# The expert numbers of a PEER selection: from 128 one-column lookups to step comparisons on 64 columns

## The chip, the cores and the metric

The kernel runs on one core of a Trainium2 chip. The metric is the device time of one execution in microseconds (us); smaller is better. The kernel before was run three times for it: 3990.93 us is the median, 3989.17 the lowest and 3995.62 the highest.

## The reference, cut to what matters

The model is a decoder of two layers for 512 tokens of width 1024. Each layer has a mixer (HGRN2 and S5 branches) and then a PEER part: eight heads per token choose 16 of 16384 experts each, an expert is one row of a table U and one of a table V. The choice is what the change touches:

```
s = einsum('thpd,hpnd->thpn', q, keys32)              # 128 scores for each of two key halves
s1_v, s1_i = top_k(s[:, :, 0, :], 16)
s2_v, s2_i = top_k(s[:, :, 1, :], 16)
cand_v = s1_v[..., :, None] + s2_v[..., None, :]      # 256 candidates per head
cand_i = s1_i[..., :, None] * 128 + s2_i[..., None, :]
top_v, top_j = top_k(cand_v, 16)
idx = take_along_axis(cand_i, top_j)                  # the expert numbers
gate = softmax(top_v)
act = gelu(einsum('thkd,td->thk', u_tab[idx], hb))
out = einsum('thkd->td', gate * act, v_tab[idx])
```

## The kernel before, in words

The 512 tokens are handled in four blocks of 128, tokens on partitions. For the first 384 tokens the kernel does not gather expert rows: it multiplies the tokens by the whole table U and by the whole table V, as dense matmuls, and weighs the products between them with a matrix of 128 by 128 gates per token, which is nearly all zero. For the last 128 tokens it gathers the chosen rows by indirect DMA, issued on POOL (`gather`, L957), 128 times from U and 128 times from V, through three buffers.

A layer's PEER part (`peer`, L819) has these steps in the order of the program:

- Scores (`scores`, L833): for 16 key halves a matmul, then `top16` on VectorE for each block of tokens, which leaves the 16 best values in `sv` and their numbers in `sx`.
- Selection (`select(tb)`, L847): of the 256 pairs per head only 50 can be among the best 16; `CAND` lists how many second-half partners each of the 16 first-half ranks has (16, 8, 5, 4, 3, 2, 2, 2 and eight times 1), `COFF` where each group begins. `cv` holds the 50 sums of scores, `ci` the 50 sums of codes (first number times 128 plus second number). `top16` finds the 16 best of `cv` per head and their positions `tj`. Then, for each of 8 heads and 16 choices, one instruction (L876) compares the numbers 0 to 49 with the position, multiplies by the 50 codes and accumulates: the result is the chosen code. Shift and mask part it into the two numbers, which go to `fx` with the gates. The block of the gathered tokens is selected first, then the other three in turn.
- Builds (`build`, L907): for four tokens at a time, VectorE makes one-hot matrices P and Q in fp16 (L921, L923, L927), eight matmuls multiply them (L933, L934), and ACT copies the 4 gate matrices to `stg`; each 48 tokens are stored to DRAM (`sW`, L939). There are 32 builds per block, 96 in all.
- U (`dense_U`, L795): 128 times a 512 KB piece of table U is loaded, split on ACT and VectorE into two parts (`whi` L114, `wlo` L116), and multiplied in 24 matmuls (L132 to L134) with the tokens; the result goes to DRAM (`sA`). In the program, one U follows every second build, and the rest of U comes after the builds. Behind each U stands one step of the gathers: a gather, then a product with the token's row on VectorE (L967), later the sum over V rows (`gacc`, L978).
- V (L1041 to L1043): 128 pieces of table V are loaded and split in the same way; `sA` and `sW` are read back, multiplied on VectorE (L1028), and fed to 24 matmuls each, which accumulate in all eight PSUM banks. In the first layer the tables of the next layer's mixer are prepared beside this (`next_layer`).

The order on each engine isn't the order of the program. The kernel is scheduled by a planner that simulates the engines with its own costs and takes, on each engine, what is ready and comes first in the program; U's and V's loads and splits are moved ahead by a fixed priority. Every engine then works through its own list in that order, and waits where an input isn't there.

Of the kernel before, what the change touches and what calls it, by code (L numbers as in the profile page):

```python
# [4 lines left out]
F32 = mybir.dt.float32  # L5
F32R = mybir.dt.float32r
F16 = mybir.dt.float16
I32 = mybir.dt.int32
U32 = mybir.dt.uint32
U8 = mybir.dt.uint8  # L10
AF = mybir.ActivationFunctionType
OP = mybir.AluOpType
# [4 lines left out]
T = 512  # L17
# [19 lines left out]
CAND = [16, 8, 5, 4, 3, 2, 2, 2] + [1] * 8  # L37
NCAND = sum(CAND)
COFF = [sum(CAND[:i]) for i in range(16)]


def trunk(tc, a, dbg=None, layers=L, n_i2=128):
    nc = tc.nc
    V, S, G, TE = nc.vector, nc.scalar, nc.gpsimd, nc.tensor
    uid = [0]

    def nm(s):
        uid[0] += 1
        return f"{s}{uid[0]}"
# [3 lines left out]
    cst = ctx.enter_context(tc.tile_pool(name="cst", bufs=1))  # L53
# [6 lines left out]
    def ptile(shape, tag):  # L60
        return psp.tile(shape, F32, tag=tag, name=nm(tag), bufs=PB[tag])
# [16 lines left out]
    iof = cst.tile([128, 128], F32, name="iof")  # L78
# [16 lines left out]
    V.tensor_tensor(eye4, ident[:, 0:32], ident[:, 32:64], op=OP.add)  # L95
    V.tensor_tensor(eye4, eye4, ident[:, 64:96], op=OP.add)
    V.tensor_tensor(eye4, eye4, ident[:, 96:128], op=OP.add)


    def load_raw(src, eng=None):  # L100
# [299 lines left out]
    def s5_maps(l, sm, keep, pool, tags):  # L400
        E = V
        br, bi, tmp = (pool.tile([128, 32, 16], F32, tag=t, name=nm(t), bufs=1) for t in tags)
        nc.sync.dma_start(br, a["bre"][l])
        nc.sync.dma_start(bi, a["bim"][l])
        bb = [keep.tile([128, 32, 16], F32, name=nm("bb")) for _ in range(2)]
        zrb, zib = (z[:, :, None].to_broadcast([128, 32, 16]) for z in sm["z"])
        E.tensor_tensor(bb[0], zrb, br, op=OP.mult)
        E.tensor_tensor(tmp, zib, bi, op=OP.mult)
        E.tensor_tensor(bb[0], bb[0], tmp, op=OP.subtract)
        E.tensor_tensor(bb[1], zrb, bi, op=OP.mult)  # L410
        E.tensor_tensor(tmp, zib, br, op=OP.mult)
        E.tensor_tensor(bb[1], bb[1], tmp, op=OP.add)
        cc_ = [keep.tile([128, 32, 16], F32, name=nm("cc")) for _ in range(2)]
        nc.sync.dma_start(cc_[0], a["cre"][l])
        nc.sync.dma_start(cc_[1], a["cim"][l])
        S.activation(cc_[1], cc_[1], AF.Copy, scale=-1.0)
        sm.update(bb=bb, cc=cc_)
# [7 lines left out]
    def pack_tile(pool):  # L425
        t = pool.tile([128, PK], F32, name=nm("pk"))
        G.memset(t, 0.0)
        return t
# [55 lines left out]
    def mixer(l, h):  # L484
# [4 lines left out]
        fx = hctx.enter_context(tc.tile_pool(name=f"fx{l}", bufs=1))  # L489
# [9 lines left out]
        if l == 0:  # L499
            s5_maps(l, sm, fx, hp, ("w1", "w2", "w3"))  # L500
            pk0 = pack_tile(fx)
        dcol = fx.tile([128, 32], F32, name=nm("dcol"))
        for j in range(4):
            nc.sync.dma_start(dcol[32 * j:32 * j + 32, :], a["dsk"][l])
# [235 lines left out]
        fx = mctx.enter_context(tc.tile_pool(name=f"gx{l}", bufs=1))  # L740
# [78 lines left out]
    def peer(l, h, rows, gp):  # L819
        pctx = ExitStack()  # L820
        rp = pctx.enter_context(tc.tile_pool(name=f"rp{l}", bufs=2))
# [4 lines left out]
        def top16(val, idx, src, work):  # L826
            V.max(val[:, 0:8], src)
            V.max_index(idx[:, 0:8], val[:, 0:8], src)
            V.match_replace(work, val[:, 0:8], src, NEG)
            V.max(val[:, 8:16], work)  # L830
            V.max_index(idx[:, 8:16], val[:, 8:16], work)

        def scores(p, ps):  # L833
# [9 lines left out]
            for tb in range(NB):  # L843
                wk = rp.tile([128, 128], F32, tag="wk", name=nm("wk"))
                top16(sv[:, tb, p], sx[:, tb, p], s[:, tb], wk)

        def select(tb):  # L847
            val = sv[:, tb].rearrange("p (h s) k -> p h s k", s=2)
            idf = rp.tile([128, 16, 16], F32, tag="idf", name=nm("idf"), bufs=1)
            V.tensor_copy(idf, sx[:, tb])  # L850
            idv = idf[:].rearrange("p (h s) k -> p h s k", s=2)
            V.tensor_scalar(idv[:, :, 0, :], idv[:, :, 0, :], 128.0, None, op0=OP.mult)
            cv = rp.tile([128, 8, NCAND], F32, tag="cv", name=nm("cv"), bufs=1)
            ci = rp.tile([128, 8, NCAND], F32, tag="ci", name=nm("ci"), bufs=1)
            for src, dst in ((val, cv), (idv, ci)):
                for r in range(5):
                    n = CAND[r]
                    V.tensor_tensor(dst[:, :, COFF[r]:COFF[r] + n], src[:, :, 0, r:r + 1].to_broadcast([128, 8, n]),
                                    src[:, :, 1, 0:n], op=OP.add)
                V.tensor_tensor(dst[:, :, COFF[5]:COFF[8]].rearrange("p h (r b) -> p h r b", b=2),  # L860
                                src[:, :, 0, 5:8, None].to_broadcast([128, 8, 3, 2]),
                                src[:, :, 1, None, 0:2].to_broadcast([128, 8, 3, 2]), op=OP.add)
                V.tensor_tensor(dst[:, :, COFF[8]:], src[:, :, 0, 8:16],
                                src[:, :, 1, 0:1].to_broadcast([128, 8, 8]), op=OP.add)
            tv = rp.tile([128, 8, 16], F32, tag="tv", name=nm("tv"), bufs=1)
            tj = rp.tile([128, 8, 16], U32, tag="tj", name=nm("tj"), bufs=1)
            for hh in range(8):
                wk = rp.tile([128, NCAND], F32, tag="wk2", name=nm("wk2"))
                top16(tv[:, hh], tj[:, hh], cv[:, hh], wk)
            tf = rp.tile([128, 8, 16], F32, tag="tf", name=nm("tf"), bufs=1)  # L870
            V.tensor_copy(tf, tj)
            code = rp.tile([128, 8, 16], F32, tag="code", name=nm("code"), bufs=1)
            for hh in range(8):
                for k in range(16):
                    jk = rp.tile([128, NCAND], F32, tag="jk", name=nm("jk"))
                    V.scalar_tensor_tensor(jk, iof[:, 0:NCAND], tf[:, hh, k:k + 1], ci[:, hh], op0=OP.is_equal,  # L876
                                           op1=OP.mult, accum_out=code[:, hh, k:k + 1])
            cint = rp.tile([128, 128], I32, tag="cint", name=nm("cint"), bufs=1)
            V.tensor_copy(cint, code[:].rearrange("p h k -> p (h k)"))
            ii = rp.tile([128, 2, 128], I32, tag="ii", name=nm("ii"), bufs=1)  # L880
            V.tensor_scalar(ii[:, 0], cint, 7, None, op0=OP.logical_shift_right)
            V.tensor_scalar(ii[:, 1], cint, 127, None, op0=OP.bitwise_and)
            fx = rp.tile([128, 3, 128], F32, tag="fx", name=nm("fx"), bufs=1)
            V.tensor_copy(fx[:, 0:2], ii)

            gv = fx[:, 2].rearrange("p (h k) -> p h k", h=8)
            V.tensor_tensor(gv, tv, tv[:, :, 0:1].to_broadcast([128, 8, 16]), op=OP.subtract)
            S.activation(fx[:, 2], fx[:, 2], AF.Exp)
            zs = rp.tile([128, 8], F32, tag="zs", name=nm("zs"), bufs=1)
            V.tensor_reduce(zs, gv, axis=mybir.AxisListType.X, op=OP.add)  # L890
            V.reciprocal(zs, zs)
            V.scalar_tensor_tensor(gv, gv, GATE, zs[:, :, None].to_broadcast([128, 8, 16]), op0=OP.mult, op1=OP.mult)
            if tb == NB - 1:
                return fx
            pt = ptile([128, 3, 128], "pc")
            for i in range(3):
                TE.transpose(pt[:, i], fx[:, i], ident)
            st = rp.tile([128, 2, 128], F16, tag="slot", name=nm("slot"))
            S.activation(st, pt[:, 0:2], AF.Copy)
            gh = rp.tile([128, 2, 128], F16, tag="gh", name=nm("gh"))  # L900
            V.tensor_copy(gh[:, 0], pt[:, 2])
            V.tensor_tensor(gh[:, 1], pt[:, 2], gh[:, 0], op=OP.subtract)
            return st, gh
# [96 lines left out]
        for p in range(16):  # L1000
            scores(p, first[3 + p] if p < 3 else dense(a["wq"][l, p], h))
        steps[0] = gather_steps(select(NB - 1))
        for tb in range(NB - 1):
            sel = select(tb)
# [48 lines left out]
        def spilled(i):  # L1053
            w = wv(i)
            A = vp.tile([128, TD], F32, tag="A", name=nm("A"), bufs=3)
            nc.sync.dma_start(A, sA[l][i])
            return w, gated(i, A)

        n_end = max(n1 - VB, 0)
        for i in range(n_end):  # L1060
            w, g = spilled(i)
# [31 lines left out]
    for k in ("adab", "n1g", "n2g", "glub"):  # L1093
        sh = a[k].shape
# [12 lines left out]
    for j in range(J):  # L1107
        m = cst.tile([128, 2], F32, name=nm("m"))
        for k in range(2):
            t = ad0.tile([128, D], F32, tag="ada", name=nm("ada"))  # L1110
# [35 lines left out]
    for l in range(layers):  # L1146
        h = norm_mod(gain1[l], shift1[l], ssq, G if l == 0 else None)
# [72 lines left out]
```

## Time and profile before

| | |
|---|---|
| median of three runs | 3990.93 us |
| the profiled execution | 3988.25 us, of which 3986.4 us are the span from the first to the last instruction |
| TensorE (PE) busy | 3737.9 us, 94% |
| VectorE (DVE) busy | 3270.8 us, 82% |
| ScalarE (ACT) busy | 1577.6 us, 40% |
| GpSimd (POOL) busy | 883.7 us, 22% |
| mean granted TensorE clock | 0.967 |
| L876 in all | 1024 pairs, 223.9 us for the comparisons and 81.8 for the accumulator reads |

Busy times count an instruction from its start to its end. Instructions of one engine overlap by a little, since one starts while the one before drains, so the sum of two groups can exceed the time in which they ran. Matmul ends are modelled: a TensorE that is busy throughout may still do fewer matmuls per microsecond than in another stretch, so counts (x) are read beside busy times. [...]

### The profile page before, as it was taken

To read this page: it belongs to the slowest core of one execution; us is meant where nothing else is said; L and a number is where in the kernel's file an instruction comes from. 1 tells how busy PE (TensorE), PEld (TensorE's weight loads), DVE (VectorE), ACT (ScalarE), POOL (GpSimd) and SP (SyncE) were. 2 spreads that over 40 slices of the span, in tenths; PEclk is the share of its full clock that TensorE was granted. 3 is DMA by queue.
4 is the path that set the end of the run, shared out by engine and by line. 5 is a ranking of instruction groups with operands and counts; after the bars stand their busy time and mean duration, and the time that the engine had idled before them with its cause. 6 is when DMAs were issued, how large, how long until landed. Compare 5 with 4: busy or idle time off the path is not lost.

```text
span 3986.4 us, 62595 instructions
## 1 busy us (share of the span) xinstructions
PE 3737.9 (94%) x21878; PEld 3500.6 (88%) x21878; DVE 3270.8 (82%) x9052; ACT 1577.6 (40%) x2510; POOL 883.7 (22%) x1139
## 2 busy tenths in 40 slices
PE   6999999999999766889999999999999998699998
PEld 5888878999999766888998888789999997699998
DVE  6998787999898889988757777869998988778874
ACT  3454543334343323334434444533334433233332
POOL 7454100022222433341000000000232223332210
PEclk9999999999999778999999999999999998799999
DMA  5222372488898899998743343723799998999984
GB/s 198 71 65 79 117 230 91 131 296 304 321 320 314 289 327 343 364 345 292 273 146 110 120 141 124 253 87 119 270 316 319 319 321 305 324 345 345 348 296 132
DMA packets 371212, 947.55 MB, mean 238 GB/s; under 512 B 36096, under 2 KB 187712, under 8 KB 368848
## 3 DMA queue, kind: packets, MB, share of 16 engines
q1 hardware_dynamic: 250144, 572.74, 42.5%
q0 software_dynamic: 73952, 268.56, 19.6%
q10 hardware_dynamic: 46800, 102.26, 6.7%
q8 instruction: 172, 2.82, 0.3%
q14 instruction: 144, 1.18, 0.1%
HBM read 814.44 MB, written 128.97 MB: 237 GB/s over the span
## 4 chain that ended last, share of the span: by engine, by line
PE 65%; DVE 16%; DMA 11%; issue 4%; ACT 2%; POOL 2%; ACTq 0%; SPq 0%; DVEq 0%; POOLq 0%
PE mm L133 11%; PE mm L132 11%; PE mm L134 11%; DVE wlo L116 3%; DMA gr<-v,idi 3%; PE mm L1042 2%; PE mm L1043 2%; PE mm L1041 2%; DMA gr<-ur,idi 2%; DVE jk L876 2%; DMA ada<-ada 2%; PE pa L1043 2%; PE pa L1042 2%; PE pb L1042 2%; PE pb L1043 2%
## 5 line engine op out<-in xcount | busy, mean ns | idle before, releaser
L114 ACT ACTIVATE whi<-raw 128x1024 fp32r<-128x1024 f32 x688 | 728.6, 1060 | 1354.1 <-PE mm L133 772.8
L133 PE MATMUL mm<-alo,whi 128*128 128x384 f32 (+1 forms) x3360 | 1213.7, 362 | 13.6 <-DVE alo L123 13.4
L134 PE MATMUL mm<-ahi,wlo 128*128 128x384 f32 (+1 forms) x3360 | 1214.1, 362 | 9.4 <-DVE wlo L116 9.1
L132 PE MATMUL mm<-ahi,whi 128*128 128x384 f32 (+1 forms) x3360 | 1213.0, 363 | 6.4 <-ACT ahi L229 5.6
L116 DVE TENSOR_TENSOR wlo<-raw,whi 128x1024 fp32r<-128x1024 f32 x688 | 840.2, 1222 | 254.5 <-ACT whi L114 239.1
L133 PEld LDWEIGHTS mm<-alo,whi 128*128 128x128 f32 x3360 | 636.0, 189 | 64.2 <-DVE alo L123 14.7
L134 PEld LDWEIGHTS mm<-ahi,wlo 128*128 128x128 f32 x3360 | 636.2, 189 | 61.1 <-DVE wlo L116 12.4
L132 PEld LDWEIGHTS mm<-ahi,whi 128*128 128x128 f32 x3360 | 636.6, 190 | 56.8 <-ACT ahi L229 7.1
L957 POOL DMA_INDIRECT gr<-ur,idi x256 | 278.1, 1086 | 1438.1 <-DVE jk L876 384.0
L957 POOL DMA_INDIRECT gr<-v,idi x256 | 362.2, 1415 | 662.7 <-DVE gacc L978 526.0
L978 DVE SCALAR_TENSOR_TENSOR gacc<-gr,gate,gacc 128x1024 f32<-128x1024 f32 x254 | 324.5, 1278 | 51.1 <-DMA gr<-v,idi 50.3
L1041 PE MATMUL mm<-gh,whi 128*128 128x384 f32 x768 | 227.3, 343 | 112.1 <-ACT whi L114 48.4
L967 DVE SCALAR_TENSOR_TENSOR gr<-gr,rows 128x1024 f32<-128x1024 f32 x256 | 311.0, 1217 | 17.6 <-DMA gr<-ur,idi 17.1
L1042 PE MATMUL mm<-gl,whi 128*128 128x384 f32 x768 | 260.9, 342 | 11.1 <-DVE gl L1032 11.0
L1043 PE MATMUL mm<-gh,wlo 128*128 128x384 f32 x768 | 255.9, 339 | 0.2 <-DVE wlo L116 0.2
L1041 PEld LDWEIGHTS mm<-gh,whi 128*128 128x128 f32 x768 | 142.5, 191 | 116.1 <-ACT gh L1030 66.0
L933 PE MATMUL pa<-Q,P 128*128 128x128 f16 x768 | 197.7, 296 | 43.7 <-DVE Q L927 41.1
L1030 ACT ACTIVATE gh<-A 128x384 fp32r<-128x384 f32 x256 | 132.1, 519 | 268.7 <-DVE A L1028 216.8
L876 DVE SCALAR_TENSOR_TENSOR jk<-iof,tf,ci 128x50 f32<-128x50 f32 x1024 | 223.9, 263 | 0.0
L935 ACT ACTIVATE stg<-pa 128x512 f32<-128x512 f32 x192 | 114.4, 598 | 223.3 <-PE pa L934 191.0
L934 PE MATMUL pa<-Q,P 128*128 128x128 f16 x768 | 187.9, 295 | 1.0
L1028 DVE TENSOR_TENSOR A<-A,W 128x384 f32<-128x384 f32 x256 | 139.2, 552 | 57.1 <-DMA A<-sA 52.0
(410 smaller groups left out, 6573.9 us busy)
## 6 DMA issues: line engine op xcount, KB each, us to landing
raw<-u SPq DMA_DIRECT2D x256, 512.0 KB
raw<-v SPq DMA_DIRECT2D x256, 512.0 KB
raw<-win SPq DMA_DIRECT2D x112, 512.0 KB
ada<-ada SPq DMA_DIRECT2D x96, 512.0 KB
sA<-uo ACTq DMA_DIRECT2D x256, 192.0 KB
sW<-stg ACTq DMA_DIRECT2D x64, 768.0 KB
A<-sA SPq DMA_DIRECT2D x256, 192.0 KB
W<-sW SPq DMA_DIRECT2D x64, 768.0 KB
```

The lines of the kernel that those rows point to most:

```text
L114: S.activation(hi, raw, AF.Copy)
L116: V.tensor_tensor(lo, raw, hi[:].bitcast(F32), op=OP.subtract)
L132: TE.matmul(ps, hi[:, w], ah, start=(j == 0), stop=False)
L133: TE.matmul(ps, hi[:, w], al, start=False, stop=False)
L134: TE.matmul(ps, lo[:, w], ah, start=False, stop=(j == J - 1))
L876: V.scalar_tensor_tensor(jk, iof[:, 0:NCAND], tf[:, hh, k:k + 1], ci[:, hh], op0=OP.is_equal, op1=OP.mult, accum_out=code[:, hh, k:k + 1])
L957: G.indirect_dma_start(out=g[:], out_offset=None, in_=tab, in_offset=bass.IndirectOffsetOnAxis(ap=ids[:, s_:s_ + 1], axis=0))
L967: V.scalar_tensor_tensor(g, g, 1.0, rows, op0=OP.mult, op1=OP.mult, accum_out=dot[:, s_:s_ + 1])
L978: V.scalar_tensor_tensor(acc_, g, gate[:, s_:s_ + 1], acc_, op0=OP.mult, op1=OP.add)
L1041: TE.matmul(ps, w[0][:, c], g[0], start=first, stop=False)
L1042: TE.matmul(ps, w[0][:, c], g[1], start=False, stop=False)
L1043: TE.matmul(ps, w[1][:, c], g[0], start=False, stop=last)
```

## The change

The 128 lookups per block, the codes `ci` and the integer arithmetic behind them go. Instead the two expert numbers are worked out from the position j of a chosen candidate among the 50. For 64 columns at once (four heads of 16 choices; two calls per selection), in fp16:

- the first-half rank is the number of group beginnings (COFF) that j has reached; the first number is the first entry plus the sum, over the 15 steps, of (j >= COFF) times the difference of neighbouring entries;
- the second-half rank is j minus the sum of the sizes (CAND) of the groups passed; the second number is the sum, over 16 ranks, of (rank equal) times the entry.

The sums over 15 or 16 rows are trees of additions that halve the number of rows. Constants are kept as pairs of equal values, so that a repeated operand still has runs of two fp16 values. The working rows are taken from the buffers of tag `s`, which the scores use before. The copy `second` is on ACT, all else on VectorE; the 30 memsets of the constants are on POOL, ahead of the first mixer.

```diff
+    thr = cst.tile([128, 15, 2], F16, name="thr")
+    cnd = cst.tile([128, 15, 2], F16, name="cnd")
+    rnk = cst.tile([128, 16, 2], F16, name="rnk")
+
+    def rank_tables():
+        V.tensor_copy(rnk, iof[:, 0:16, None].to_broadcast([128, 16, 2]))
+        for r in range(1, 16):
+            G.memset(thr[:, r - 1], float(COFF[r]))
+            G.memset(cnd[:, r - 1], float(CAND[r - 1]))
...
+        def ranks(iv, j, o0, o1):
+            j = j.rearrange("p h k -> p (h k)")
+            def work(n):
+                return rp.tile([128, T], F32, tag="s", name=nm("s"))[:].bitcast(F16)[:, 0:64 * n].rearrange(
+                    "p (r x) -> p r x", r=n)
+            def pairs(t, n):
+                return t[:, :, None, :].to_broadcast([128, n, 32, 2])
+            def twos(w):
+                return w.rearrange("p r (a b) -> p r a b", b=2)
+            def total(w, n, o):
+                while n > 2:
+                    m = (n + 1) // 2
+                    V.tensor_tensor(w[:, 0:n - m], w[:, 0:n - m], w[:, m:n], op=OP.add)
+                    n = m
+                V.tensor_tensor(o, w[:, 0], w[:, 1], op=OP.add)
+            def gate_rows(w, t, n):
+                sh = [128, n * 4, 8, 2]
+                v = w.rearrange("p r (h a b) -> p (r h) a b", h=4, b=2)
+                V.tensor_tensor(v, v, t[:].rearrange("p r h b -> p (r h) b")[:, :, None, :].to_broadcast(sh), op=OP.mult)
+            step = rp.tile([128, 15, 4, 2], F16, tag="step", name=nm("step"), bufs=1)
+            two = [128, 4, 15, 2]
+            V.tensor_tensor(step[:].rearrange("p r h b -> p h r b"), iv[:, :, 0, 1:16, None].to_broadcast(two),
+                            iv[:, :, 0, 0:15, None].to_broadcast(two), op=OP.subtract)
+            second = rp.tile([128, 16, 4, 2], F16, tag="second", name=nm("second"), bufs=1)
+            S.activation(second[:].rearrange("p r h b -> p h r b"), iv[:, :, 1, :, None].to_broadcast([128, 4, 16, 2]),
+                         AF.Copy)
+            ge, w = work(15), work(15)
+            V.tensor_tensor(twos(ge), twos(j[:, None].to_broadcast([128, 15, 64])), pairs(thr, 15), op=OP.is_ge)
+            V.tensor_tensor(twos(w), twos(ge), pairs(cnd, 15), op=OP.mult)
+            r2 = rp.tile([128, 64], F16, tag="r2", name=nm("r2"), bufs=1)
+            total(w, 15, r2)
+            V.tensor_tensor(r2, j, r2, op=OP.subtract)
+            gate_rows(ge, step, 15)
+            total(ge, 15, o0)
+            o0 = o0.rearrange("p (h k) -> p h k", h=4)
+            V.tensor_tensor(o0, o0, iv[:, :, 0, 0:1].to_broadcast([128, 4, 16]), op=OP.add)
+            eq = work(16)
+            V.tensor_tensor(twos(eq), twos(r2[:, None].to_broadcast([128, 16, 64])), pairs(rnk, 16), op=OP.is_equal)
+            gate_rows(eq, second, 16)
+            total(eq, 16, o1)
...
-            V.tensor_scalar(idv[:, :, 0, :], idv[:, :, 0, :], 128.0, None, op0=OP.mult)
-            for src, dst in ((val, cv), (idv, ci)):
+            for src, dst in ((val, cv),):
...
-            for hh in range(8):
-                for k in range(16):
-                    jk = rp.tile([128, NCAND], F32, tag="jk", name=nm("jk"))
-                    V.scalar_tensor_tensor(jk, iof[:, 0:NCAND], tf[:, hh, k:k + 1], ci[:, hh], op0=OP.is_equal,
-                                           op1=OP.mult, accum_out=code[:, hh, k:k + 1])
-            V.tensor_copy(cint, code[:].rearrange("p h k -> p (h k)"))
-            V.tensor_scalar(ii[:, 0], cint, 7, None, op0=OP.logical_shift_right)
-            V.tensor_scalar(ii[:, 1], cint, 127, None, op0=OP.bitwise_and)
-            V.tensor_copy(fx[:, 0:2], ii)
+            jf = rp.tile([128, 8, 16], F16, tag="jf", name=nm("jf"), bufs=1)
+            V.tensor_copy(jf, tj)
+            for hf in range(2):
+                ranks(idv[:, 4 * hf:4 * hf + 4], jf[:, 4 * hf:4 * hf + 4], fx[:, 0, 64 * hf:64 * hf + 64],
+                      fx[:, 1, 64 * hf:64 * hf + 64])
```

## Rows read from the trace of the kernel before

**Rows 1.** The page, part 1: busy us, share of the span, instructions.
```profile
PE 3737.9 (94%) x21878; PEld 3500.6 (88%) x21878; DVE 3270.8 (82%) x9052; ACT 1577.6 (40%) x2510; POOL 883.7 (22%) x1139
```

**Rows 2.** Table of stretches, first layer's PEER part: busy us and counts, clock, DMA share, GB/s.
```profile
770.00:820.00 50.00, 50.00 (x290) 50.00 (x289) 49.97 (x376) 20.60 (x29) 0.00 (x0) 1.00 0.59 174
820.00:925.00 105.00, 103.63 (x594) 102.28 (x593) 98.53 (x428) 37.23 (x52) 35.72 (x35) 1.00 0.95 333
925.00:1085.00 160.00, 159.78 (x991) 152.94 (x990) 145.61 (x448) 66.21 (x98) 41.86 (x39) 1.00 0.88 309
...
1350.00:1397.00 47.00, 25.12 (x176) 19.16 (x174) 43.09 (x96) 14.06 (x24) 22.02 (x12) 0.55 0.73 262
1397.00:1422.00 25.00, 0.21 (x2) 0.16 (x1) 10.58 (x14) 1.33 (x3) 8.42 (x8) 0.50 0.95 333
1422.00:1550.00 128.00, 87.71 (x467) 86.87 (x468) 117.59 (x306) 36.62 (x52) 52.82 (x40) 0.81 0.93 327
1550.00:1850.00 300.00, 266.54 (x1449) 260.17 (x1449) 269.80 (x529) 114.42 (x171) 99.36 (x70) 0.96 0.96 345
```

**Rows 3.** The same table for the second layer, around the start of its V stage.
```profile
3404.00:3429.00 25.00, 0.89 (x7) 0.60 (x6) 10.63 (x10) 0.60 (x1) 9.18 (x9) 0.50 0.96 350
3429.00:3962.00 533.00, 532.41 (x3066) 532.42 (x3067) 399.49 (x486) 195.00 (x255) 123.13 (x98) 1.00 0.88 310
```

**Rows 4.** Stretches, instructions on P alone: TensorE, weight loads, VectorE, clock, DMA.
```profile
925.00:1085.00 160.00, 36.30 (x245) 25.81 (x246) 13.06 (x32) 1.00 0.88 309
...
1350.00:1397.00 47.00, 25.12 (x176) 19.16 (x174) 8.21 (x21) 0.55 0.73 262
```

**Rows 5.** Stretches, instructions on jk alone (L876 and its accumulator reads): VectorE, clock, DMA.
```profile
770.00:820.00 50.00, 28.43 (x268) 1.00 0.59 174
820.00:925.00 105.00, 27.93 (x251) 1.00 0.95 333
...
1085.00:1130.00 45.00, 13.87 (x128) 1.00 0.96 326
...
1285.00:1310.00 25.00, 6.22 (x60) 1.00 0.91 307
```

**Rows 6.** Timeline of VectorE in the first selection: start, us.
```profile
786.58 0.23 DVE L863 TENSOR_TENSOR cv<-sv 128x64 f32<-128x64 f32 x1
786.72 0.27 DVE L876 SCALAR_TENSOR_TENSOR jk<-iof,tf,ci 128x50 f32<-128x50 f32 x1
...
786.91 0.28 DVE L876 SCALAR_TENSOR_TENSOR jk<-iof,tf,ci 128x50 f32<-128x50 f32 x1
```

**Rows 7.** Timeline of VectorE at the start of a build.
```profile
1306.00 0.42 DVE L921 TENSOR_TENSOR P<-io,slot 128x512 f16<-128x512 f16 x1
1306.33 0.42 DVE L923 TENSOR_TENSOR Qo<-io,slot 128x512 f16<-128x512 f16 x1
```

**Rows 8.** Timeline of VectorE at the kernel's start, a chain.
```profile
4.88 0.29 DVE L91 TENSOR_TENSOR m<-m,gt 128x128 f32<-128x128 f32 x1
5.21 0.29 DVE L92 SCALAR_TENSOR_TENSOR masks<-xo,m 128x128 uint8<-128x128 int32 x1
```

**Rows 9.** Stretches: line L116 alone (VectorE); then tile rows alone (VectorE, ACT).
```profile
770.00:820.00 50.00, 14.66 (x12) 1.00 0.59 174
820.00:925.00 105.00, 29.26 (x24) 1.00 0.95 333
...
820.00:925.00 105.00, 39.22 (x64) 0.00 (x0) 1.00 0.95 333
```

**Rows 10.** Instructions on tile gacc from 2600 us on.
```profile
L978 DVE SCALAR_TENSOR_TENSOR gacc<-gr,gate,gacc x127: 1266/1279/1286, 3332.9 to 3839.0; 128x1024 f32<-128x1024 f32 x127
```

**Rows 11.** Timeline of POOL: its first wait for data, and a small memset.
```profile
22.23 1.35 POOL L286 TENSOR_TENSOR s5s<-s5s 128x32 f32<-128x32 f32 x2 [15.21 <-DMA s5s<-are]
...
92.03 0.11 POOL L469 MEMSET pk<- 128x4 f32 x1
```

**Rows 12.** Waits of ACT, 740 to 1350 us: total, times, longest.
```profile
ACT uo L798 <- DMA sA<-uo: 16.4, 6, 8.6
```

## The prediction before the run

> **What bounds the kernel now.** I read three views in this order: the page's totals, the table of stages of the layers' expert parts (whole, then for one tile at a time), and the timeline with single instructions. The page has TensorE busy for 94% of the span and VectorE for 82% [rows 1], so a shorter VectorE instruction is worth something only where TensorE stands still. The table of stages shows where that is [rows 2]. From 770 to 1350 us TensorE is busy practically all the time: 50.00 of 50, 103.63 of 105, 159.78 of 160. [...]
>
> [...] From 925 to 1085 us TensorE does 245 build matmuls, 31 builds, beside (991-245)/24 = 31 U matrices [rows 2, 4]: one build per U. From 1350 to 1397 it does 176 of them, 22 builds [rows 4], and no U is left to do: the U work ran out before the builds. In that tail VectorE is busy 43.09 of the 47 us [rows 2], so TensorE goes at VectorE's pace. Then 25 us pass in which the last weights are stored to DRAM and read back, and the V stage starts.
>
> Why do 22 builds remain? Because TensorE has stretches in which it does only U: 770 to 925, 1085 to 1130 and 1285 to 1310, in which VectorE works out the expert numbers of the next 128 tokens, and is full (49.97 of 50 and 98.53 of 105 in the first two [rows 2]). The compare-and-sum instruction at L876 takes 28.43 and 27.93 us of these two, 13.87 of the 45 and 6.22 of the 25 [rows 5]. So this line sets when builds begin, and thereby how many remain when U ends.
>
> **The change, part by part.** One selection now has 128 pairs at L876, each an instruction of 50 columns and its accumulator read; pairs start 0.19 us apart (786.72, 786.91) [rows 6], 24.3 us. Of the instructions that go beside them, the nearest row is a 64-wide addition, which holds the engine 0.14 us (786.58 to 786.72 [rows 6]): one column per cycle of 0.96 GHz, 0.067, and 0.07 fixed. By that the seven additions for the candidates' codes, 24 to 128 columns, cost 0.9, and the scaling, the cast to integers, shift, mask and the cast back, 128 columns and one of 256, 1.2. Removed: 26.4 us.
>
> Added are two calls of `ranks`, 20 VectorE instructions each. The nearest rows for fp16 with a repeated operand are the build's comparisons: 512 columns start 0.33 us apart [rows 7], which is two columns per cycle (0.267) and the same 0.07. At that rate the five big ones (960 or 1024 columns) take 2.91 us, the three trees 2.32, the three small ones 0.43 (the step differences, whose repeated operand can't be packed, at one column per cycle): 5.7 us per call. That is the lower bound, reached if every instruction can start while the one before it drains. The upper one is a chain: where an instruction reads the result of the one before, it starts 0.04 us after that one's end (4.88 + 0.29 to 5.21 [rows 8]): 0.33 us for 128 columns, where the distance of independent ones would be 0.07 + 0.133 = 0.20. 0.13 more for each of 20 is 2.6, so 8.3 us. A selection pays 11.3 to 16.6. I take 13.9, the middle, because the planner has other instructions to put between (the U weights' remainder, the gathers' products) but the chain is long. Net: 26.4 - 13.9 = 12.5 us less VectorE work per selection, bounds 9.8 to 15.1; 50 per layer, 100 in both.
>
> [...]
>
> Where this falls: the first selection (770 to 820) shares VectorE with the U weights' remainder, 14.66 of 50 us [rows 9]; it shortens by 12.5/0.71 = 18 us. The second (820 to 925) shares it with that (29.26 of 105) and with the gathers' products (39.22): 12.5/0.35 = 36. The last two are partly done beside builds, and only their rest stands in the gaps of 45 and 25 us; 12.5 less covers nearly all of 13.87, and all of 6.22 [rows 5]: 36 and 18. In sum up to 108 us less U-only time, 26 U at 4.14 us (290 matmuls / 24 in 50 us [rows 2]), beside which as many builds find room. The tail has 22; so it goes, with a margin of four.
>
> What that is worth: TensorE's own work stays. A build beside U costs it (160 - 31 x 4.14)/31 = 1.0 us [rows 2, 4], in the tail 47/22 = 2.14; 22 x 1.14 = 25 us. The 25 us of store and reload remain, because nothing proves that builds end before U does. So both V stages start 25 us earlier. In the second layer TensorE is full from there on [rows 3], and the last expert row is added at 3839 [rows 10], 120 us before the stage ends: the 25 us are kept. In the first layer DMA is busy 0.93 and 0.96 of the time from 1422 to 1850 and TensorE stands still for 40 and 33 us there [rows 2]: it is limited by the gathers and by the next layer's preparation. The gathers start 18 us earlier, as the first selection does. I count 20 of the 25.
>
> The rest: two ACT copies per selection, hidden in ACT's idle time. Thirty POOL memsets at up to 0.11 us [rows 11] are 3.3 us; in POOL's wait of 15.2 us for its first data [rows 11] they cost nothing, behind it up to 3.3, as the first mixer's tables then come later. I take nothing and keep 3 for the range. VectorE's table copy is 0.2 us.
>
> The sum: 3986.4 span - 25 - 20 = 3941. The profiled execution took 3988.25 and the median is 3990.93, so 2.7 goes on the execution's time and 4.5 on the span: 3946, rounded to 3945.
>
> **The rivals.**
> Builds end well before U does, and the store and reload hide as well: the margin of four builds, and any build done quicker than one per U, speak for it, the planner's steady pace of one per U against. The gain is 50 in the second layer and 40 in the first: 3901.
>
> Pairs don't pack: the new operands repeat runs of two fp16 values, the measured ones runs of four [rows 7]. At one column per cycle a call streams 8.3 us instead of 4.3, a selection costs 19.3 to 24.6, and 4.4 is saved instead of 12.5. Then 108 x 0.36 = 39 us less U-only time, some 10 builds, 11 us per layer: 3969. [...]
>
> The first layer gives all back to DMA: 3990.9 - 25 = 3966.
>
> Slower: a wait on ACT. The new copy `second` stands in ACT's order, and `gate_rows(eq, second)` on VectorE waits for it, two per selection; behind that wait stand the next U's `wlo` and the gathers' products, and TensorE and POOL wait for these. ACT itself waits up to 8.6 us for the stores of U's output [rows 12]; I take that as the most by which the copy is late. Over 2 x 8 = 16 waits of w each, 100 - 16w is left of the 100 us: from w = 6.3 it is slower. At 8.6 us, VectorE has 38 more, and by the same rate (45 per 100) 17 us are added: 4008. Against it: the copy's input is ready some ten instructions before it is needed.
>
> **How the numbers follow.** Forecast 0.50 (3925 to 3962); hidden store 0.17; pairs unpacked 0.13; given back 0.08; slower 0.08; no movement, because the planner's order undoes it, 0.04. The range: down to 3888 for the hidden store with the lower bound of the chains, up to 3983, which takes in the unpacked pairs with their upper bound and the memsets. Within 0.2% (8 us, about what this kernel's measurement can tell) are the last case and edges of the unpacked one: 0.08; slower 0.08; faster 0.84.
>
> **What would show it.** Right: L876 gone; a call's big instructions near 0.57 us apart; the first build near 870 us; hardly any build after the last U; V stages 25 us earlier. Wrong: instructions of 1.0 us; VectorE idle before `gate_rows` behind ACT; the tail still there; TensorE idle between 770 and 1350; or more idle time in the first V stage.

## The result and the profile after

The changed kernel takes 3945.06 us, the median of four runs (3938.24 to 3950.8), against 3993.27 for the kernel before (3989.17 to 3998.01): a ratio of 0.9881, 95% interval 0.9869 to 0.9894. The medians are 48 us apart; the profiled executions, 3988.25 before and 3950.8 after, are 37.5 apart, since the one after was the slowest of its four. What follows counts in the profiled ones.

The page after, part 1 (busy us, share of the span 3949.0, instructions), beside [rows 1]:

```profile
PE 3741.0 (95%) x21878; PEld 3509.6 (89%) x21878; DVE 3157.4 (80%) x7229; ACT 1577.8 (40%) x2526; POOL 892.1 (23%) x1169
```

VectorE works 113 us less, and TensorE's busy time stands: what went is TensorE's idle time. The table of stretches of the first layer, columns as in [rows 2] (busy us and counts of TensorE, weight loads, VectorE, ACT and POOL, then clock, DMA share, GB/s):

```profile
740.00:870.00 130.00, 127.58 (x733) 127.07 (x732) 121.70 (x496) 55.31 (x78) 28.42 (x22) 0.99 0.72 242
870.00:1085.00 215.00, 214.84 (x1331) 205.46 (x1330) 194.16 (x461) 87.85 (x134) 57.47 (x51) 1.00 0.90 313
1085.00:1277.00 192.00, 190.93 (x1232) 180.70 (x1231) 159.37 (x332) 79.26 (x122) 39.78 (x39) 1.00 0.84 296
1277.00:1300.00 23.00, 17.90 (x89) 17.51 (x88) 11.36 (x16) 5.52 (x8) 7.11 (x6) 0.85 0.99 389
1300.00:1387.00 87.00, 84.39 (x487) 84.07 (x485) 56.93 (x62) 31.02 (x44) 35.44 (x27) 1.00 0.92 323
1387.00:1402.00 15.00, 0.22 (x1) 0.22 (x2) 8.51 (x17) 0.80 (x2) 7.04 (x6) 0.55 1.04 373
```

The same stretches for the instructions on P alone (TensorE, weight loads, VectorE), beside [rows 4]:

```profile
870.00:1085.00 215.00, 48.22 (x320) 33.53 (x320) 17.18 (x41) 1.00 0.90 313
1085.00:1277.00 192.00, 64.06 (x448) 47.81 (x448) 22.95 (x54) 1.00 0.84 296
1277.00:1387.00 110.00, 0.07 (x1) 0.00 (x0) 0.00 (x0) 0.97 0.94 337
```

The builds begin at 870 and no longer at 925, and end at 1277 and no longer at 1397. From 870 to 1085 there are 320/8 = 40 beside (1331-320)/24 = 42 U; from 1085 to 1277 there are 56 beside (1232-448)/24 = 33: 1.7 per U. Behind the last build 24 U remain, (89+487)/24. Before, it was the other way round: 22 builds without a U. The tail is gone, and the hole of 72 us (1350 to 1422, 25 busy) has become one of 15 (1387 to 1402), with a smaller one at 1277.

The second layer, beside [rows 3]:

```profile
3270.00:3300.00 30.00, 24.43 (x129) 24.12 (x129) 16.59 (x22) 9.01 (x13) 8.68 (x7) 0.89 0.92 335
3300.00:3371.00 71.00, 71.00 (x412) 71.00 (x411) 45.95 (x49) 24.67 (x35) 30.43 (x23) 1.00 0.95 339
3371.00:3391.00 20.00, 1.03 (x5) 0.71 (x4) 10.94 (x12) 2.55 (x5) 8.74 (x7) 0.60 0.99 362
3391.00:3924.00 533.00, 533.00 (x3072) 533.00 (x3070) 407.81 (x492) 193.56 (x253) 128.51 (x106) 1.00 0.88 316
```

What TensorE waited for in the kernel after (total us, times, longest), first from 700 to 1440 us, then from 2600 to 3450:

```profile
PE mm L1089 <- ACT gh L1078: 17.4, 1, 17.4
PE mm L142 <- ACT uo L810: 6.3, 3, 5.1
...
PE mm L1089 <- ACT gh L1078: 19.0, 1, 19.0
PE mm L142 <- ACT uo L810: 8.8, 3, 5.6
```

L1089 is the first matmul of the V stage, L810 the gelu that empties a U matrix's PSUM. Before, these were the rows from 700 to 1440 us (L1041 is the V stage's first matmul; the releaser named for it is the load that landed last):

```profile
PE mm L1041 <- DMA s5s<-ldt: 24.8, 1, 24.8
PE pa L933 <- DVE Q L927: 20.5, 10, 6.8
```

Both waits after are new in kind: before, builds waited for VectorE, and the V stage's first matmul was late because the gate weights were. Their last store, in the chain of waits before (start, us, what):

```profile
1400.03 13.04 DMA sW<-stg
```

Where each V stage ends is seen from the matmuls that add the gathered rows, first and last start; L1072 is before, L1120 after:

```profile
L1072 PE MATMUL mm<-ident,gacc x12: 270/275/275, 2041.5 to 3952.1; 128*128 128x128 f32 x12
```

```profile
L1120 PE MATMUL mm<-ident,gacc x12: 271/275/275, 2021.0 to 3913.4; 128*128 128x128 f32 x12
```

The first layer's end comes 20.5 us earlier, the second's 38.7, of which 18.2 are its own.

VectorE in the first selection, start and us, with two of the new instructions on 960 columns:

```profile
771.16 0.64 DVE L892 TENSOR_TENSOR s<-jf,thr 128x960 f16<-128x960 f16 x1
771.72 0.28 DVE L938 TENSOR_REDUCE zs<-fx 128x8 f32<-128x128 f32 x1
...
773.30 0.65 DVE L893 TENSOR_TENSOR s<-s,cnd 128x960 f16<-128x960 f16 x1
773.87 0.19 DVE L939 RECIPROCAL zs<-zs 128x8 f32<-128x8 f32 x1
```

The next, independent instruction starts 0.56 and 0.57 us later. Against the 0.33 us of 512 columns [rows 7], 448 more columns cost 0.23 to 0.24 us, or 0.52 ns each, which leaves some 0.06 us that don't depend on the columns. The pairs pack as the runs of four in [rows 7] do.

### The profile page after: what moved, and what is told of

It reads as the page before. It is cut to its first block, busy times and chain, and to the rows that moved or that the text cites. A ratio compares the mean times of both kernels' runs of the same rounds, so it can differ in the third digit from the quotient of the medians.

```text
span 3949.0 us, 60873 instructions
## 1 busy us (share of the span) xinstructions
PE 3741.0 (95%) x21878; PEld 3509.6 (89%) x21878; DVE 3157.4 (80%) x7229; ACT 1577.8 (40%) x2526; POOL 892.1 (23%) x1169
## 4 chain that ended last, share of the span: by engine, by line
PE 73%; DMA 9%; DVE 7%; issue 7%; POOL 3%; ACT 1%; ACTq 0%; SPq 0%; DVEq 0%; POOLq 0%
PE mm L142 12%; PE mm L143 12%; PE mm L144 12%; DMA gr<-v,idi 3%; PE mm L1090 3%; PE mm L1089 3%; PE mm L1091 3%; PE pa L1090 2%; PE pa L1091 2%; PE pa L1089 2%; PE pb L1090 2%; PE pb L1089 2%; PE pb L1091 2%; POOL gr L1005 2%; PE pa L981 1%
## 5 line engine op out<-in xcount | busy, mean ns | idle before, releaser
L142 PE MATMUL mm<-ahi,whi 128*128 128x384 f32 (+1 forms) x3360 | 1220.2, 365 | 21.3 <-ACT uo L810 15.1
L143 PEld LDWEIGHTS mm<-alo,whi 128*128 128x128 f32 x3360 | 639.3, 190 | 64.1 <-DVE alo L133 14.3
L1005 POOL DMA_INDIRECT gr<-ur,idi x256 | 293.8, 1148 | 1467.1 <-DMA sA<-uo 696.1
L1005 POOL DMA_INDIRECT gr<-v,idi x256 | 354.0, 1383 | 651.4 <-DVE gacc L1026 490.0
L1089 PE MATMUL mm<-gh,whi 128*128 128x384 f32 x768 | 223.9, 343 | 105.8 <-ACT gh L1078 67.7
L1089 PEld LDWEIGHTS mm<-gh,whi 128*128 128x128 f32 x768 | 142.7, 191 | 109.4 <-ACT gh L1078 70.9
L1089 PE MATMUL pa<-gh,whi 128*128 128x384 f32 x512 | 174.5, 341 | 0.0
L1089 PE MATMUL pb<-gh,whi 128*128 128x384 f32 x512 | 174.4, 341 | 0.0
```

Of the source, the lines that this page charges most:

```text
L142: TE.matmul(ps, hi[:, w], ah, start=(j == 0), stop=False)
L143: TE.matmul(ps, hi[:, w], al, start=False, stop=False)
L1005: G.indirect_dma_start(out=g[:], out_offset=None, in_=tab, in_offset=bass.IndirectOffsetOnAxis(ap=ids[:, s_:s_ + 1], axis=0))
L1089: TE.matmul(ps, w[0][:, c], g[0], start=first, stop=False)
```

## The experiments

**First question: is it VectorE's time that held the builds back, in proportion?** Four kernels change that time and little else. In `e1_half`, the loop of L876 runs over half the ranks:

```diff
-                for k in range(16):
+                for k in range(8):
...
+            V.tensor_copy(code[:, :, 8:16], code[:, :, 0:8])
```

> The kernel before, with 64 of the 128 lookups of each selection left out (the codes of ranks 8 to 15 are copies of those of ranks 0 to 7), and none of the new instructions: per selection 64 x 0.19 = 12.2 us of VectorE's time less, about the 14.1 that the change took out (113 us in 8 selections). Theory, that VectorE's time alone held the builds back: about 12.2/14.1 of the change's gain of 48 us, so 3945 to 3960. Rival, that the new order of the work or the new instructions' kind (short ones, none of them with an accumulated column) brings the gain: 3975 to 3993.

Measured: 3963.12 us, ratio 0.9933 (0.9917 to 0.995).

`e2_none`, also from the kernel before:

```diff
-            for hh in range(8):
-                for k in range(16):
-                    jk = rp.tile([128, NCAND], F32, tag="jk", name=nm("jk"))
-                    V.scalar_tensor_tensor(jk, iof[:, 0:NCAND], tf[:, hh, k:k + 1], ci[:, hh], ...
+            V.scalar_tensor_tensor(code, tf, 301.0, iof[:].rearrange("p (h k) -> p h k", h=8), op0=OP.mult, op1=OP.add)
```

> The kernel before with no lookup at all (one instruction makes the code from the position, so the chosen experts are others): 24 us of VectorE's time less per selection, 1.7 times what the change took out. If the gain is in proportion to the time taken out: 3993 - 1.7 x 48 = 3912. If the change has used up what the builds' tail held, because the builds now end 110 us ahead of the U matmuls and what is left at the start of the V stage is a chain of transfers: 3930 to 3950. If less VectorE work draws other work forward that collides, not below 3950.

Measured: 3948.39 us, ratio 0.9902 (0.9885 to 0.9919).

`e3_pad`, from the kernel after:

```diff
...
+            for hh in range(8):
+                for k in range(8):
+                    jk = rp.tile([128, NCAND], F32, tag="jk", name=nm("jk"))
+                    V.scalar_tensor_tensor(jk, iof[:, 0:NCAND], tf[:, hh, k:k + 1], cv[:, hh], ...
```

> The changed kernel, with 64 of the old lookups added to each selection on scratch tiles that nothing reads: 12.3 us of VectorE's time more per selection and no other work. Theory of VectorE's time: nearly all of the gain goes, 3980 to 3992. Rival, that the gain is the new order or the chain of fewer dependent steps: 3945 to 3965.

Measured: 3989.52 us, ratio 1.0001 (0.999 to 1.0011).

`e4_nopair`, from the kernel after:

```diff
-                return t[:, :, None, :].to_broadcast([128, n, 32, 2])
+                return t[:, :, 0:1].to_broadcast([128, n, 64])
```

and the same in `gate_rows`; `twos` then leaves its operand as it is.

> The changed kernel with the constants of each group broadcast one by one along the columns instead of in pairs (the innermost step of that operand is 0): the five large instructions of each half, 10 per selection, should lose their two columns per cycle, from 0.57 to about 1.07 us apart, 5 us per selection and 40 in all. Theory of VectorE's time: (14.1 - 5) / 14.1 of 48 us are left, 3960 to 3966. If the pairs don't matter to the rate, or VectorE's time doesn't to the span: 3943 to 3950.

Measured: 3971.98 us, ratio 0.9949 (0.9932 to 0.9965). Its VectorE at the same place as above:

```profile
770.75 1.14 DVE L892 TENSOR_TENSOR s<-jf,thr 128x960 f16<-128x960 f16 x1
771.81 0.28 DVE L938 TENSOR_REDUCE zs<-fx 128x8 f32<-128x128 f32 x1
```

1.06 us apart: without pairs the same 960 columns take 0.50 us more, 1.04 ns each, half the rate.

Side by side, with VectorE's busy time from each page against 3270.8 before:

| kernel | VectorE less, us | ratio | first layer: last build, V begins, rows added (us) |
|---|---|---|---|
| before | 0 | 1 | 1397, 1421.8, 2041.5 |
| `e3_pad` | 22 | 1.0001 | 1398, 1423.6, 2036.6 |
| `e4_nopair` | 72 | 0.9949 | 1316, 1401.0, 2041.6 |
| `e1_half` | 93 | 0.9933 | 1302, 1407.4, 2036.7 |
| after | 113 | 0.9881 | 1277, 1401.8, 2021.0 |
| `e2_none` | 186 | 0.9902 | 1176, 1402.3, 2015.9 |

`e1_half` has none of the new instructions and still gains; `e3_pad` has them all and gains nothing. So it is VectorE's time, and not the new instructions or their number. But it isn't in proportion. `e2_none` shows an end: 73 us less than after and no faster, since with the tail gone V begins at 1402 in the first layer whatever VectorE saves. (Its experts are others, so its gathers read other rows; that this costs nothing is taken, not shown.) And `e4_nopair` and `e1_half` fell 6 and 3 us outside their expected ranges: the tail is gone in both, but the first layer kept little of it. In `e4_nopair` V begins 21 us earlier than before and ends at the same time. Its last gathered row is added on VectorE at 1888.0 us, after at 1859.7; the limited part of the V stage goes on longer. The rival in which the first layer gives all back thus happened in this kernel. That the later gathers are the cause was not tested by itself, and they can't be all of it: in `e5_uo_apart` and `e6_uo_apart_four` below, the last gathered row is added later still, at 1931.8 and 1973.6 us, and yet the rows are added by matmuls earlier, at 2009.2 and 1991.9. The cause stays open.

**Second question: what is the new wait at the start of the V stage?** The chain of waits of `e2_none` around it (start, us, what; L798 is the gelu of U, L1022 and L1052 loads on SyncE's queue, L1024 the product A x W):

```profile
1384.98 0.19 PE mm L133
...
1386.15 0.48 ACT uo L798
...
1386.66 4.34 DMA sA<-uo
...
1391.08 0.33 SPq L1052
...
1391.45 0.43 SPq L1022
...
1391.93 9.79 DMA A<-sA
...
1401.74 0.56 DVE A L1024
```

The load of the first A, whose data were stored 640 us before, goes out only when the last U's output has been stored. Either SyncE waits for memory, since the V stage's tiles lie where the U stage's pool was (which holds `uo`), or for data. `e5_uo_apart` moves `uo` to the gathers' pool, which stays open:

```diff
-                dense_U(l, ui[0], h, rp)
+                dense_U(l, ui[0], h, gp)
```

> The changed kernel with the U stage's output tiles (uo, still two of them) in the pool of the gathers, which stays open, and no longer in the pool that the V stage's tiles take the memory of. In the changed kernel TensorE waits 17.4 us (first layer) and 19.0 us (second) at the start of the V stage: last U matmul, gelu, store of uo, and only when that store has landed the loads of A and W. Theory A, that the loads wait because their tiles reuse the memory of the pool: both waits shrink to under 4 us, 36 us in all at most; 3905 to 3925. Theory B, that they wait for the store for the data's sake (the loads read what the stage has written, the tensor as one), or because SyncE's queue stands behind something else: the waits stay, 3940 to 3950.

Measured: 3921.69 us, ratio 0.9844 (0.9822 to 0.9865). `e7_three_uo` leaves it in place and takes `UB = 3` for 2:

> The changed kernel with three uo tiles instead of two, in their old pool. TensorE waited 14.4 us ahead of U matmuls in the first layer (6.3, 3.0 and 5.1 us) for gelus that waited for stores of uo, queued behind the stores of gate weights in the same queue; the clock fell to half in two of these stretches. If the third tile takes these waits away: 10 to 15 us per layer, 3918 to 3930. If the stretch is bounded elsewhere (VectorE's splits, the wait moves): 3940 to 3950. The wait at the start of the V stage stays, 17 to 20 us, by either theory of it.

(The 14.4 us in it were misread: the row says 6.3 us in all, 3 times, the longest 5.1; the second layer has 8.8.) Measured: 3928.6 us, ratio 0.9856 (0.9839 to 0.9872). The wait at the start of V, expected at 17 to 20 us, came out lower, at 14.5 and 14.3. `e6_uo_apart_four` has the first edit and `UB = 4`:

> The changed kernel with four uo tiles, in the gathers' pool: the two edits above together. If they are two causes that add up: both waits gone, 3890 to 3910. If one of them is no cause: as the other alone.

Measured: 3893.7 us (3880.91 to 3893.9), ratio 0.9755 (0.9734 to 0.9776): 2.45% faster than before, twice the change alone.

TensorE's waits of these two kinds, from 700 to 1440 and from 2600 to 3450. `e5_uo_apart`:

```profile
PE mm L142 <- ACT uo L810: 17.8, 9, 5.4
...
PE mm L142 <- ACT uo L810: 12.9, 5, 4.9
```

`e7_three_uo` (the releaser named for L1089 in the first layer is the load that landed last on the profile, not the one that it needs):

```profile
PE mm L1089 <- DMA s5s<-aim: 14.5, 1, 14.5
PE mm L142 <- ACT uo L810: 2.3, 1, 2.3
...
PE mm L1089 <- ACT gh L1078: 14.3, 1, 14.3
PE mm L142 <- ACT uo L810: 2.0, 1, 2.0
```

`e6_uo_apart_four` has no row of either kind in either stretch; its table of stretches shows TensorE full where the hole was:

```profile
1300.00:1400.00 100.00, 99.86 (x574) 99.53 (x573) 88.22 (x290) 46.95 (x68) 27.27 (x23) 1.00 0.95 330
1400.00:1430.00 30.00, 30.00 (x172) 30.00 (x171) 29.08 (x58) 9.02 (x14) 11.33 (x7) 1.00 0.97 346
3270.00:3440.00 170.00, 170.00 (x983) 170.00 (x982) 121.83 (x150) 62.52 (x84) 43.75 (x40) 1.00 0.94 331
```

The waits add up to 51.5 us after, 30.7 in `e5_uo_apart`, 33.1 in `e7_three_uo` and 0 in `e6_uo_apart_four`; the spans are 3949.0, 3919.5, 3925.8 and 3891.8. So 20.8, 18.4 and 51.5 us less waiting go with 29.5, 23.2 and 57.2 us less span. The profiled execution of the kernel after was its slowest, though: by the ratios the three gain 15, 10 and 50 us on the change alone, and only the last agrees with the waits by both counts. The wait at the start of V was one for memory: with `uo` elsewhere, the first load of A goes out at 1288.8 us and no longer at 1391.1, and nothing waits there. Taken away alone it gives a part back: 15.1 us of waits for `uo` became 30.7, and 11.2 of the first layer's 17.8 lie between 1300 and 1400 us, beside the V stage's loads, where there were none. That these loads keep the two `uo` tiles busy longer fits, but was not tested by itself. With four tiles both gains stand; four tiles in the old place were not tried. Only the interval of `e7_three_uo` touches that of the change alone (0.9869 to 0.9894).

`e8_before_uo_apart` makes the first edit in the kernel before:

> The kernel before with its uo tiles (two) in the gathers' pool, nothing else. There the last loads of A and W came 13.2 and 13.5 us after the last copy of a build had been stored (1400.0), 20 us after the last U matmul. Theory: in the kernel before the gate weights themselves are what is late (builds' tail), so the place of uo is worth nothing: 3985 to 3995, and the same edit gains only once the builds end early. Rival, that 20 to 25 us of the hole were this reuse already before: 3945 to 3965.

(In the trace of the kernel before, 1400.0 is when the last store of the gate weights goes out; it lands at 1413.1, and the loads go out right behind it, 63 us behind the last U matmul and not 20.) Measured: 3989.05 us, ratio 1.0004 (0.9995 to 1.0014). Its TensorE from 700 to 1440:

```profile
PE mm L1041 <- DMA A<-sA: 25.0, 1, 25.0
PE pa L933 <- DVE Q L927: 20.7, 10, 6.7
```

The tail (L933 are the builds, held by VectorE) and the 25 us behind it stand as they were. The place of `uo` cost nothing while the builds were late; the change has made it the thing that is late next.

`e11_sw_by_sync` asks whether the waits for `uo` come from ScalarE's queue:

```diff
-                    nc.scalar.dma_start(sW[l][n, :, q:q + 32], stg[0][:, q:q + 32])
+                    nc.sync.dma_start(sW[l][n, :, q:q + 32], stg[0][:, q:q + 32])
```

> The changed kernel (two uo tiles, in their old place) with the stores of the gate weights issued by SyncE's queue and no longer by ScalarE's, in which they stand ahead of the stores of uo. Theory, that TensorE's waits for uo come from uo's stores queued behind the gate weights' (four stores issued in a row, 3.9 us for one alone): as with three uo tiles, 3925 to 3935. Rival, that two uo tiles are too few in any case while gathers and loads share the DMA engines: 3940 to 3950. Second rival: SyncE's queue, which holds the U stage's weight loads, now waits for the copies ahead of each store, and TensorE starves: over 3950.

Measured: 3938.79 us, ratio 0.9878 (0.9861 to 0.9896), the same ratio as the change alone. This lies between the ranges of the theory and of its rival. The waits for `uo` became short but not few:

```profile
PE mm L142 <- ACT uo L810: 5.0, 5, 1.3
...
PE mm L142 <- ACT uo L810: 5.0, 5, 1.3
```

The longest was 5.1 and 5.6 us and is 1.3: the gate weights' stores on ScalarE's queue make the long ones. Whether by their transfers or by ScalarE's time to issue them (0.33 to 1.86 us each, four in a row) is not separated. But 10.0 of 15.1 us are left, the wait at V's start is too (17.0 and 18.1), and no gain can be told. The theory of the queue explains the waits' length and not their sum.

## Why the prediction was right, and where its steps were not

The forecast of 3945 was met, the cause that it names was confirmed, but two of its steps failed, and their errors nearly cancel. That the number is so close is luck: the builds' end as it came out is that of the rival with a gain of 90 us, and 51.5 us of waits that nobody had counted took it back: 38.5 by this estimate, against 37.4 in the span.

- **VectorE's time.** 12.5 us less per selection were predicted, 100 in all (bounds 78 to 121); the page says 113, or 14.2 per selection. With the 26.4 us taken for the part removed, a selection pays 12.2 for the new chains, less than the middle taken (13.9) and close to the lower bound (11.3), where an instruction starts before the one ahead of it has ended. In the timeline above, the planner does put others between the steps. The two of 960 columns last 0.64 and 0.65 us, but an independent successor starts after 0.56 and 0.57. The rates that the prediction prices with are in the trace before, between starts of VectorE without idle time:

```profile
785.05 1.23 DVE L116 TENSOR_TENSOR wlo<-raw,whi 128x1024 fp32r<-128x1024 f32 x1
786.19 0.09 DVE L831 MATCH_VALUE_LOAD tj<-tv,wk 128x8 f32 x1
```

1024 columns hold the engine for 1.14 us, 64 for 0.14 [rows 6]: 1.04 ns for each further column, which is the prediction's cycle, and 0.07 us that don't depend on the columns. With 0.07 taken off, the 0.33 us of 512 fp16 columns [rows 7] are 0.51 ns each.
- **Packing.** Right: 0.56 to 0.57 us, as forecast. The rival that pairs don't pack was priced at 3969; `e4_nopair`, which unpacks only the five large instructions of each call, took 3971.98. The two agree in the number alone: the rival leaves half of the tail, and in `e4_nopair` the tail is gone and the first layer gave its gain back.
- **The first build.** Predicted near 870 us, 54 us earlier than before (18 + 36); its first matmul moved from 932.1 to 875.0, 57 us.
- **One build per U: the step that failed.** The prediction took the rate of 925 to 1085 [rows 2, 4] for the planner's steady pace, and so found 26 builds of room for a tail of 22, a margin of four. The later stretch has 1.7 builds per U, and the margin is 24 U. Before, VectorE was 91% busy at the pace of one [rows 2]; after, from 1085 to 1277, it is 83% busy at the higher one. The trace before had a hint of it, in the last stretch of U that [rows 2] and [rows 4] leave out (all, then P alone):

```profile
1310.00:1350.00 40.00, 39.68 (x253) 37.13 (x252) 35.05 (x64) 16.09 (x26) 16.27 (x11) 1.00 0.90 303
...
1310.00:1350.00 40.00, 12.53 (x82) 8.67 (x83) 4.00 (x10) 1.00 0.90 303
```

These are 10 builds beside (253-82)/24 = 7 U. And the pace rises with the time that VectorE is spared: from the first build to the last, the 96 builds stand beside 78 U in `e1_half`, 75 after and 63 in `e2_none`, pauses for the selections included. The program's order, one U for every two builds, allows more.

- **Store and reload: a similar number, another reason.** "The 25 us of store and reload remain, because nothing proves that builds end before U does." They do end before, by 110 us, and the gate weights' round trip is hidden, as the rival of 3901 had it. What stands in its place is another round trip, that of the last `uo`, because of the reuse of its pool's memory (17.4 and 19.0 us). With that gone `e6_uo_apart_four` takes 3893.7; the rival had the mechanism but not the next wait. The prediction never asked what else the V stage's first load waits for; no wait of the kernel before shows it, since the builds hid it.
- **25 us per layer.** V begins 20.0 us earlier in the first layer (1421.8 to 1401.8), and in the second 39.1 in clock time (3429.6 to 3390.5), 18.6 of its own behind the first layer's 20.5. The missing 5.0 and 6.4 are what is left of several changes: the wait at V's start fell by 7.4 and 5.7 us (24.8 and 24.7 before, 17.4 and 19.0 after), and new waits of 6.3 and 8.8 stand ahead of U matmuls, which the prediction did not have. TensorE idle between 770 and 1350, a sign of being wrong by its own list, did show: 8.8 us, against 1.9 before. What the rest comes from was not worked out.
- **What the first layer keeps.** Counted 20 of 25; it kept 20.5 of 20. The reason given holds in part: the gathers do start 18 us earlier (821.0 to 803.4), but their last row is added 18 us later (1841.6 to 1859.7), and the layer lost nothing by it; why, no run shows. The second kept 18.2, all but 0.4. The sum predicted was 45; 38.7 at the last added rows and 37.4 in the span came of it, and 48 between the medians, which are further apart than the profiled executions.
- **The wait on ACT** (rival, slower) did not occur. ACT waited for VectorE instead. Instructions on the tile `second`: what ACT waited for, total and times, and who waited for VectorE's:

```profile
L889 ACT ACTIVATE second<-idf x16: 301/320/325, 760.1 to 3006.4; 128x128 f16<-128x128 f16 x16
...
  DVE idf L909: 14.7, 4
  DVE s L882: 9.9, 5
...
  ACT second L889: 9.9, 5
```

No VectorE instruction is named as waiting for `second`. The memsets were taken as nothing: the first U's gelu starts at 746.2 us, 743.9 before, and between 740.6 and 748.3 in the other kernels, so no effect of theirs can be told.

## What to carry to other kernels

When an engine off the bottleneck is relieved, price the gain by the bottleneck's idle stretch, and then ask what is late next there: which transfer, which buffer, which pool's memory the next stage takes over. A pace read from one stretch is not the planner's limit; look for the stretch in which the limiting engine has most room. An edit worth nothing before a change (1.0004) can be worth as much as the change after it, so wait lists are read anew after each change.

## What the runs showed of the hardware

- With an operand that repeats pairs of fp16 values, 960 columns took 0.56 us from start to start (after); with its innermost step at 0, 1.06 (`e4_nopair`).
- Where TensorE waited for a few microseconds, its granted clock was lower too: in the kernel after, 0.85 from 1277 to 1300, idle for 5.1 of 23 us, and 0.89 from 3270 to 3300, idle for 5.6 of 30; with four `uo` tiles all three stretches around the two V starts have 1.00.
- When the gate weights' stores left ScalarE's queue, TensorE's longest wait for `uo` fell from 5.1 us in the first layer and 5.6 in the second to 1.3 in both (`e11_sw_by_sync`), though the ratio did not change.
